# A list schedule made twice: the second pass counts due times from the first pass's tensor-engine times

## The chip, the cores and the metric

The kernel runs on one core of a Trainium2 chip. A core has a matrix engine (TensorE, "PE" in the profile; its weight loads are listed apart as "PEld"), a vector engine (DVE), a scalar engine (ACT), a general engine (POOL), and SyncE (SP), which here only issues DMA transfers. Each engine takes its own instructions in one fixed order; engines meet through semaphores. The metric is the device time in microseconds of one execution. Before the change it is 1381.08 us, the median of three runs (1380.90 to 1382.62).

## What is computed

One layer of a streaming encoder for two request groups that share weights: a prompt of 2048 rows of width 1024, and a sample batch of 8 streams with 16 new rows each, whose keys and values of 1024 past rows lie in a cache.

```
h = rms_norm(x);  z = h @ w_in                  # 1024 -> 3584 columns
u_a, v_a, g_a, q, k, v, g_b = split(z)
y_a = u_a * (tril(W_s) @ rms_norm(v_a) + b_s) * silu(g_a)     # 4 groups, chunks of 128 rows
q, k = rms_norm(q), rms_norm(k)                                # 4 heads x two halves of 64
a = softmax(q1 k1 - slope*dist) - lam * softmax(q2 k2 - slope*dist)
y_b = rms_norm(a @ v) * silu(g_b)
y = x + concat(y_a, y_b) @ w_out
```

The prompt's attention is causal in blocks of 64; the sample's sees all 1024 past rows and its own. Keys, values and the sample's v_a are outputs too.

## The kernel before, in words

All matrix products run on PE in fp32r, most of them three times: an operand is split into a rounded high part (ACT, line 481 or 648) and a low remainder (DVE, line 482 or 649), and high-high, high-low and low-high products are summed in PSUM (`mm3`, lines 491 to 494; their matmuls are recorded at line 416, transposes at line 420).

The work comes in stages, written as Python generators that are woven into one stream of instructions:

- The **main stream** (`stream`, line 771) makes the input projection: in two halves of the rows, for each of 14 blocks of weight columns, 24 matmuls of 256 columns into a tile `acc` for each 128 rows. Its rows come in through `xload` (lines 588 to 606: load, square on ACT, root on POOL, scaling on DVE at line 605) and `xpose` (transposes `x_tp`, then the split into `xT`). Its weights come in through `load_w` (lines 630 to 652): a load of 128 rows into `wraw` on SP (lines 634 to 641), a high part on ACT or POOL (line 648 or 645) and a low part on DVE (line 649). `wraw` has five buffers during the first block, `w` twelve. At the start, some forty small constants are loaded through the same SP queue: lines 463 to 468, 548 to 553 and 565 to 574.
- The **sample's attention** (`sample_attention`, line 1185) is woven into the main stream: cached keys through `skraw` (line 1103), cached values through `svraw` (line 1153), split into `sv`, which feed the products `sS` and `sO`. The loads of `svraw` have two buffers.
- **Attention A**, for the first eight row blocks of 128 (`attention`, line 990), is woven into the rest of the main stream: scores `S`, exponentials `ex` on ACT, their difference on DVE, transposes `a_tp`, a split `aT`, products `oT`.
- **Attention B**, for the other eight, is woven into the output projection `oo` (`out_stream`, line 1307), which loads `y` and `xo`. After B the last of the output projection runs alone.

The woven order in the code is not the order on the chip. At the end, `Order(tc).run()` (line 1362) takes all instructions and makes a **list schedule**. It goes through modelled time. For each engine it keeps the instructions whose inputs are ready, and takes the one with the lowest rank; `cost` (line 188) gives modelled durations, a DMA is modelled as 2.5 us plus its bytes, and buffers are taken and freed as the tiles' users finish. The order found for each engine is then fixed with dependencies (lines 394 to 397), so on the chip each engine follows it whatever happens.

The ranks come from `deadlines` (line 229). First every instruction gets a time `when`: the sum of the modelled PE durations ahead of it in the code's order, as if PE ran that order without a gap. A PE instruction's rank is that time. Any other instruction's due time starts at `when` plus 15 us (`LATE`), and then, going backwards, it is drawn to its users' due times less its own duration (3.1 us for a DMA) and a hop between engines; the reuse of a buffer counts as a user. SP's order of DMAs comes from the same ranks.

## Time and profile before

| | |
|---|---|
| median of 3 runs | 1381.08 us |
| profiled execution, its own time | 1381.83 us |
| its span, first to last instruction | 1380.1 us |
| instructions | 27913 |
| PE busy | 1347.1 us, 9892 matmuls and transposes |
| DVE, ACT, POOL busy | 925.7, 791.2, 452.1 us |
| moved by DMA | 183.05 MB, 133 GB/s in the mean |

The profiled execution lies 1.73 us above its span, and 0.75 us above the median of the runs. In the windows of time that are shown below, each engine has the time that it was busy and, in brackets, how many instructions it started; "PEclk" is the TensorE clock granted, 1.00 being full. In the list of waits, the columns are the total in us, how many, and the longest. Rows of the timeline give the start and the length of a merged group of like instructions, and in square brackets how long the engine was idle before it and what ended that.

### The profile page before, as it was taken

How to read it: one execution, taken by the hardware profiler on the slowest of the kernel's cores; microseconds unless marked ns; L12 is line 12 of the kernel's file. 1: busy time of each engine (PE TensorE's matmuls, PEld its weight loads, DVE VectorE, ACT ScalarE, POOL GpSimd, SP SyncE). 2: the span in 40 equal slices, each digit the busy share in tenths (PEclk: the TensorE clock that was granted, in tenths of full speed). 3: DMA queues.
4: the chain of work that ended last, by engine and by line, in shares of the span. 5: the costliest groups of instructions: out<-in, count | busy, mean ns of one | idle time of the engine just before them, and what ended most of it. 6: DMA issues, size and time to landing. Idle time of an engine off the chain costs nothing.

```text
span 1380.1 us, 27913 instructions
## 1 busy us (share of the span) xinstructions
PE 1347.1 (98%) x9892; PEld 1260.5 (91%) x9892; DVE 925.7 (67%) x2286; ACT 791.2 (57%) x1778; POOL 452.1 (33%) x624
## 2 busy tenths in 40 slices
PE   5999999999999999999999999999999999999998
PEld 5999999999998999899999999998788888888887
DVE  4532338878777796678889775433889897887721
ACT  4433337766565785556676654223777776776620
POOL 2151530101010121656442323021565555454400
PEclk9999999999999999999999999999999999999999
DMA  6533334554445576635453325226646543442223
GB/s 213 178 83 102 83 76 130 174 153 135 142 124 151 157 226 187 173 93 157 108 148 100 98 66 157 77 73 214 187 144 180 140 133 107 145 131 81 84 89 104
DMA packets 209244, 183.05 MB, mean 133 GB/s; under 512 B 21104, under 2 KB 167024, under 8 KB 209104
## 3 DMA queue, kind: packets, MB, share of 16 engines
q1 hardware_dynamic: 199280, 155.17, 38.1%
q0 software_dynamic: 9824, 26.09, 7.0%
q8 instruction: 78, 1.28, 0.4%
q14 instruction: 62, 0.51, 0.1%
HBM read 130.86 MB, written 42.47 MB: 126 GB/s over the span
## 4 chain that ended last, share of the span: by engine, by line
PE 89%; DMA 4%; ACT 3%; DVE 2%; issue 1%; SPq 1%; POOL 0%; ACTq 0%; DVEq 0%
PE acc L416 44%; PE oo L416 13%; PE S L416 9%; PE oT L416 7%; PE a_tp L420 4%; PE sS L416 2%; PE sk_tp L420 2%; PE sO L416 2%; PE y_tp L420 1%; DMA svraw<-in_cache_v_dram 1%; PE mix L416 1%; PE x_tp L420 1%; DMA wraw<-in_w_in_dram 1%; PE k_tp L420 1%; ACT sa L1142 1%
## 5 line engine op out<-in xcount | busy, mean ns | idle before, releaser
L416 PE MATMUL acc<-w,xT 128*128 128x256 f32 x5376 | 715.3, 283 | 3.6 <-DVE w L649 1.8
L416 PEld LDWEIGHTS acc<-w,xT 128*128 128x128 f32 x5376 | 675.6, 190 | 13.8 <-DVE w L649 2.3
L416 PE MATMUL oo<-wo,yT 128*128 128x512 f32 x816 | 231.7, 400 | 1.3 <-ACT yT L481 1.3
L416 PE MATMUL S<-kT,qT 128*128 128x512 f32 (+3 forms) x688 | 186.5, 361 | 2.2 <-DVE sst L911 2.1
L915 ACT ACTIVATE ex<-ex,sst 128x128 f32<-128x128 f32 (+15 forms) x128 | 153.9, 1203 | 41.1 <-DVE sst L911 40.2
L416 PEld LDWEIGHTS oo<-wo,yT 128*128 128x128 f32 x816 | 146.5, 188 | 26.6 <-ACT yT L481 1.8
L416 PE MATMUL oT<-aT,v 128*128 128x256 f32 x864 | 150.7, 293 | 0.2 <-ACT aT L481 0.2
L649 DVE SCALAR_TENSOR_TENSOR w<-wraw,normg,w 128x256 fp32r<-128x256 f32 x224 | 105.5, 496 | 57.9 <-ACT w L648 56.5
L911 DVE CUSTOM_DVE_ANT_0 ex<-S,dist,sst 128x512 f32<-128x512 f32 (+2 forms) x192 | 123.6, 652 | 29.0 <-PE S L416 27.8
L648 ACT ACTIVATE w<-wraw,normg 128x256 fp32r<-128x256 f32 x220 | 104.4, 505 | 57.3 <-DMA wraw<-in_w_in_dram 40.3
L416 PEld LDWEIGHTS S<-kT,qT 128*128 128x128 f32 x688 | 112.6, 189 | 18.1 <-DVE sst L911 6.1
L416 PEld LDWEIGHTS oT<-aT,v 128*128 128x128 f32 x864 | 120.8, 189 | 4.5 <-ACT aT L481 0.5
L481 ACT CAST aT<-a_tp 128x512 fp32r<-128x512 f32 (+1 forms) x144 | 79.7, 561 | 65.3 <-PE a_tp L420 63.3
L482 DVE TENSOR_TENSOR aT<-a_tp,aT 128x512 fp32r<-128x512 f32 (+1 forms) x144 | 93.6, 658 | 27.6 <-ACT aT L481 25.7
L911 DVE CUSTOM_DVE_ANT_0 ex<-S,dist 128x512 f32<-128x512 f32 (+3 forms) x128 | 79.2, 629 | 21.4 <-PE S L416 16.5
L488 POOL TENSOR_SCALAR vst<-vst 128x2 f32<-128x2 f32 (+1 forms) x36 | 9.0, 250 | 257.3 <-ACT vn L743 256.4
L420 PE MATMUL a_tp<-ident,ex 128*128 128x128 f32 x544 | 88.6, 274 | 1.3 <-DVE ex L927 0.9
L420 PEld LDWEIGHTS a_tp<-ident,ex 128*128 128x128 f32 x544 | 64.7, 140 | 13.1 <-DVE aT L482 2.5
L931 POOL TENSOR_TENSOR ex<-ex 128x1024 f32<-128x1024 f32 (+4 forms) x32 | 58.7, 1849 | 23.8 <-ACT ex L930 23.7
L482 DVE TENSOR_TENSOR sv<-svraw,sv 128x512 fp32r<-128x512 f32 (+1 forms) x72 | 50.3, 700 | 22.4 <-ACT sv L481 21.6
L481 ACT CAST sv<-svraw 128x512 fp32r<-128x512 f32 (+1 forms) x72 | 44.3, 618 | 32.6 <-DMA svraw<-in_cache_v_dram 15.0
L927 DVE SCALAR_TENSOR_TENSOR ex<-ex,sst 128x1024 f32<-128x1024 f32 (+4 forms) x64 | 62.1, 970 | 0.9
(144 smaller groups left out, 1901.1 us busy)
## 6 DMA issues: line engine op xcount, KB each, us to landing
wraw<-in_w_in_dram SPq DMA_DIRECT2D x160, 128.0 KB, 2.9
skraw<-in_cache_k_dram SPq DMA_DIRECT2D x64, 256.0 KB, 2.9
svraw<-in_cache_v_dram SPq DMA_DIRECT2D x64, 256.0 KB, 3.0
kT<-k_scr POOLq DMA_DIRECT2D x20, 512.0 KB, 5.2
vraw<-out_dram SPq DMA_DIRECT2D x36, 256.0 KB, 3.1
y<-y_scr SPq DMA_DIRECT2D x34, 256.0 KB, 2.9
out_dram<-xo SPq DMA_DIRECT2D x34, 256.0 KB, 2.2
wraw<-in_w_in_dram SPq DMA_DIRECT2D x128, 64.0 KB, 2.4
```

The source lines that it names most:

```text
L416: pe.last = nc.tensor.matmul(*a, **k).ins
L420: pe.last = nc.tensor.transpose(*a, **k).ins
L481: act.copy(hi, src)
L482: (lo_eng or dve).tensor_tensor(out=lo, in0=src, in1=f(hi), op=ALU.subtract)
L488: pool.tensor_scalar(out=ms, in0=ms, scalar1=1.0, scalar2=EPS, op0=ALU.mult, op1=ALU.add)
L648: act.activation(w[:, 0], r, AF.Copy, scale=normg[:, kc:kc + 1])
L649: dve.scalar_tensor_tensor(out=w[:, 1], in0=r, scalar=normg[:, kc:kc + 1], in1=f(w[:, 0]), op0=ALU.mult, op1=ALU.subtract)
L911: dve.tensor_tensor_reduce(out=ex[c][:, a:b], in0=s, in1=dist[:, off + a:off + b], scale=SLOPES[h], scalar=prev[c], op0=ALU.add, op1=ALU.m ...
L915: act.activation(ex[c][:, :w], ex[c][:, :w], AF.Exp, bias=prev[c], scale=-1.0, accum_out=st[:, c, 6:7])
L927: dve.scalar_tensor_tensor(out=p0, in0=p1, scalar=st[:, 1, 7:8], in1=p0, op0=ALU.mult, op1=ALU.add)
L931: pool.tensor_tensor(out=p0, in0=p1, in1=p0, op=ALU.add)
L1142: act.activation(a[r:r + 32], p[c1], AF.Copy, scale=st[c1, 6:7])
```

## The change

`Order(tc).run()` is called twice, each time on a new `Order`. The first call makes the schedule as before, keeps for every instruction the modelled time `at` at which it was taken, and returns these times instead of fixing an order. The second call gets them as `when`: a PE instruction's rank is now its modelled start in the first schedule, and every other instruction's due time starts from its own start in the first schedule plus 15 us, and is drawn back from the PE starts of the first schedule as before. Only the second schedule's order is fixed. No instruction, tile, buffer or transfer is added or removed; the costs, the slacks and the weaving are as before.

```diff
-    def deadlines(self, cost, reach):
-
-        N, t, when = self.nodes, 0.0, []
-        for n in N:
-            when.append(t)
-            if n.engine == self.PE:
-                t += cost[n.idx][1]
+    def deadlines(self, cost, reach, when):
+
+        N = self.nodes
         due = [x if n.engine == self.PE else x + self.LATE for n, x in zip(N, when)]
...
-    def run(self):
+    def run(self, when=None):
...
-        rank = self.deadlines(cost, reach)
+        first_pass = when is None
+        if first_pass:
+            t, when = 0.0, []
+            for n in N:
+                when.append(t)
+                if n.engine == self.PE:
+                    t += cost[n.idx][1]
+        rank = self.deadlines(cost, reach, when)
+        at = [0.0] * len(N)
...
-            n = N[i]
+            n, at[i] = N[i], t
...
+        if first_pass:
+            return at
...
-    Order(tc).run()
+    Order(tc).run(Order(tc).run())
```

## The prediction

> **What bounds the kernel now.** I read the page first:

> ```profile
> span 1380.1 us, 27913 instructions
> PE 1347.1 (98%) x9892; PEld 1260.5 (91%) x9892; DVE 925.7 (67%) x2286; ACT 791.2 (57%) x1778; POOL 452.1 (33%) x624
> ```

> PE sets the time. The change neither adds nor removes a PE instruction, so all it can touch is the 1380.1 - 1347.1 = 33.0 us in which PE is idle, and what short losses the busy time hides. The second view is the windows, cut by stage:

> ```profile
> 0.00:50.00 50.00, 34.70 (x242) 33.52 (x243) 23.87 (x55) 25.21 (x49) 10.83 (x29) 0.93 0.71 220
> 50.00:200.00 150.00, 150.00 (x1268) 150.00 (x1267) 57.11 (x129) 52.60 (x107) 61.69 (x64) 1.00 0.34 95
> 400.00:500.00 100.00, 97.26 (x776) 93.59 (x775) 78.90 (x194) 68.37 (x170) 13.37 (x25) 1.00 0.51 151
> 500.00:600.00 100.00, 95.44 (x749) 91.15 (x748) 66.54 (x147) 61.42 (x138) 39.95 (x52) 1.00 0.65 183
> 600.00:750.00 150.00, 150.00 (x1209) 146.52 (x1207) 128.85 (x337) 99.76 (x267) 72.60 (x118) 1.00 0.43 117
> 750.00:800.00 50.00, 48.54 (x381) 46.61 (x379) 39.61 (x110) 29.09 (x81) 14.48 (x31) 1.00 0.42 112
> 930.00:1000.00 70.00, 65.92 (x379) 54.65 (x379) 40.67 (x106) 37.29 (x67) 28.43 (x35) 1.00 0.65 202
> 1050.00:1340.00 290.00, 290.00 (x1757) 251.86 (x1757) 219.58 (x542) 190.69 (x330) 135.02 (x158) 1.00 0.42 123
> 1340.00:1380.10 40.10, 36.07 (x176) 29.18 (x174) 8.65 (x15) 4.30 (x11) 1.40 (x4) 1.00 0.28 95
> ```

> The second number is PE's busy time. Idle: 15.30 us in the first 50, 4.03 in the last 40, 2.74 and 4.56 in the sample's stage and at the start of attention A (400 to 600), 1.46 at 750 to 800, 4.08 at the turn to attention B (930 to 1000); the windows left out hold the other 0.9. Three long stretches, 590 us together, have none. The third view is what PE waited for:

> ```profile
> PE x_tp L420 <- DVE x L605: 9.3, 2, 7.2
> PE sO L416 <- ACT sv L481: 3.2, 2, 2.3
> PE x_tp L420 <- DVE neglam L474: 3.1, 1, 3.1
> PE q_tp L420 <- DMA qraw<-q_scr: 2.5, 2, 1.3
> PE S L416 <- DVE sst L911: 2.1, 4, 1.4
> PE acc L416 <- DVE w L649: 1.8, 1, 1.8
> PE acc L416 <- ACT w L648: 1.7, 1, 1.7
> ```

> They are single accidents of 1 to 3 us, each a late feed; only the first 7.2 us, until the first rows have arrived, is out of any order's reach.

> **The change, part by part.** Both passes run while the program is built, so the second costs the chip nothing, and all counts stay. What moves is the order on every engine, SP's DMA queue and POOL's included. A rank matters only against the other ranks on its engine, so the question is where the first schedule left the code's order. If it did not, the second pass repeats the first. The numbers of the instructions in the program give the code's order: 3342 of the main stream's `acc` matmuls stand ahead of the first `S` of attention A, 3381 ahead of its first `oT`. PE ran more (windows up to these two starts, `acc` alone):

> ```profile
> 0.00:566.50 566.50, 457.37 (x3437) 433.51 (x3437) 23.34 (x60) 41.01 (x98) 0.99 0.50 146
> 0.00:589.66 589.66, 475.24 (x3570) 450.16 (x3570) 23.34 (x60) 42.74 (x101) 0.99 0.50 146
> ```

> That is 95 and 189 `acc` early; at 150/1268 = 0.118 us each, 11 and 22 us. From 566 us on, everything that feeds attention A is ranked some 20 us too urgent against everything that feeds `acc`. By the same count the sample's first key transposes, at 203 us, are some 14 us behind the code. From 50 to 200, 800 to 930 and 1050 to 1340 the two orders agree within a few us. So the second pass has something to correct at three places.

> **(a) The head.** The code puts the transposes of row tiles 0 to 3 ahead of the first `acc`. The chip did otherwise:

> ```profile
> 9.31 0.47 SPq L548 DMA_DIRECT2D qkg<-in_q_norm_g_dram  x1
> 9.39 1.13 POOL L645 TENSOR_SCALAR w<-wraw,normg 128x256 fp32r<-128x256 f32 x2 [0.57 <-DMA wraw<-in_w_in_dram]
> 12.10 0.69 DVE L482 TENSOR_TENSOR xT<-x_tp,xT 128x512 fp32r<-128x512 f32 x1 [1.30 <-ACT xT L481]
> 13.22 0.35 SPq L593 DMA_DIRECT2D x<-in_x_prompt_dram  x1
> 14.37 2.06 DVE L649 SCALAR_TENSOR_TENSOR w<-wraw,normg,w 128x256 fp32r<-128x256 f32 x5
> 14.95 3.51 SPq L553 DMA_DIRECT2D bias_s<-in_sgu_b_dram  x4
> 16.19 4.43 PE L416 MATMUL acc<-w,xT 128*128 128x256 f32 x29
> 22.60 0.43 SPq L574 DMA_DIRECT2D ws<-in_sgu_w_dram  x1
> 23.14 1.40 SPq L634 DMA_DIRECT2D wraw<-in_w_in_dram  x3
> 23.73 1.06 PE L420 MATMUL x_tp<-ident,x 128*128 128x128 f32 x8 [3.10 <-DVE neglam L474]
> 26.54 0.79 PE L416 MATMUL acc<-w,xT 128*128 128x256 f32 x2 [1.75 <-ACT w L648]
> ```

> The first five weight tiles carry 29 `acc` at 16.19; then PE starves, first for row tile 3 (3.10 us), then for weight tiles 5 to 7 (1.75 us). Those are issued only at 23.14: their buffers come free when line 649 has read the first five (14.37 to 16.43), and eleven constants stand in front. From 9.31 to 23.03 SP issued 19 constants and two row tiles, 0.65 us each on the chip against the schedule's 0.40. In the first pass tiles 0 to 3 outrank these weights throughout; in the second the weights are due by the first pass's `acc`, which runs before tile 3. Line 649 can then go ahead of the row tiles' work on DVE, from 10.52 (the end of the POOL row) at the earliest, up to 3.85 us sooner. I take half of that, 1.9 us, which is 4 or 5 places in the schedule's SP queue, some 3 us on the chip: the 1.75 us vanish. After this gap PE also ran slow:

> ```profile
> 26.00:28.00 2.00, 1.46 (x7) 1.47 (x8) 1.75 (x4) 0.48 (x1) 0.47 (x1) 0.50 0.81 232
> 28.00:30.00 2.00, 2.00 (x11) 2.00 (x10) 1.46 (x3) 1.47 (x3) 0.10 (x1) 0.50 0.90 268
> 30.00:32.00 2.00, 2.00 (x13) 2.00 (x13) 1.18 (x3) 1.95 (x4) 0.67 (x2) 0.61 0.80 287
> 32.00:34.00 2.00, 2.00 (x19) 2.00 (x19) 1.15 (x3) 0.00 (x0) 0.08 (x1) 1.00 0.88 328
> ```

> 24 matmuls between 28 and 32 instead of 38: 14 x 0.105 = 1.5 us, and about 0.5 more before 28; 2.0 us hang on the gap, of which I take half. [...] Head: -1.75 - 1.0 = **-2.8 us**. Bounds: -6.9 if both waits and the slow clock go (3.10 + 1.75 + 2.0); +3.5 if four more constants like the `bias_s` row get ahead of a load that PE needs, which the changed due time of constants (their own early start plus 15 us, instead of the place in the code plus 15 us) could do.

> **(b) Attention A, 560 to 800.** PE's 1.8 us wait for a weight tile falls there, beside waits of attention itself (`S`, `q_tp`). The re-ranking should remove most of the first and may lengthen the others: **-1.6**, bounds -6.0 (all of the 4.56 and 1.46) and +2.3 (one new wait as long as the longest for `sv`). Attention, now less urgent, may fall further behind, but its scores end well before the main stream; first row `S`, second `acc`:

> ```profile
> 850.00:900.00 50.00, 0.00 (x0) 0.00 (x0) 0.00 (x0) 1.00 0.31 89
> 900.00:950.00 50.00, 36.74 (x307) 36.49 (x305) 1.25 (x3) 4.32 (x10) 1.00 0.49 158
> ```

> Some 50 us and more of `acc` hide a later end; without them each us of lag would cost up to one.

> **(c) The turn to attention B.** 4.08 us idle, from four kinds of wait; by the count, the output stream runs ahead of the code there by up to 20 us. I take a quarter, **-1.0**, bounds -4.1 and +2.3.

> **(d) New accidents in the sample's stage.** Here SP's order decides:

> ```profile
> 423.35 1.37 SPq L762 DMA_DIRECT2D y_scr<-ya  x3
> 424.82 0.85 SPq L1153 DMA_DIRECT2D svraw<-in_cache_v_dram  x2
> 428.59 0.50 PE L416 MATMUL sO<-sv,saT 128*128 128x512 f32 x1 [2.32 <-ACT sv L481]
> ```

> One value load issued behind stores costs PE 2.32 us. Ranks between weights, stores and sample loads shift by up to the 14 us above at the stage's start and by little later. A third of the 9.2 us of four such accidents, less the 1.6 that may as well go: **+1.4**, bounds -3.2 and +9.2.

> Sum: -2.8 - 1.6 - 1.0 + 1.4 = -4.0 us. Against the profiled execution, 1381.83 - 4.0 = 1377.8; it lay 0.75 above the median, so 1377.1 us in the terms of the runs: **1377**.

> **The rivals.** *No change* (1381, within 2.8 us, which is 0.2% and about what this kernel's runs can tell): the re-ranking stays inside slack. For it: 590 us without idle, ACT 57% and DVE 67% busy, twelve `w` buffers. Its extreme is that the second schedule repeats the first in all but the three places and the accidents there merely change names. *More than forecast* (about 1369): the head's whole 6.9 and half of the idle in (b) and (c), 5.1, go; against it, PE waited for tile 3 until 23.73 though its load had gone out at 13.22, as soon as a buffer was free, and an order can hardly issue it sooner. *Slower, by the sample's loads* (1387): where the sample is behind the code, its loads lose rank to weights and stores; SP's queue is strict, `svraw` has two buffers, and each load issued 4 us late costs 2.3 us. Four such make +9.2, less 3 of the gains: +6. It decides from three new waits on; one in the trace shows that the stage is open to it, and that only few of the 64 cache loads hit PE speaks against. [...] *Slower, by the head's constants* (1385): the +3.5 above decides if it also meets the slow clock.

> **How the numbers follow.** Forecast, 1371 to 1378: 0.40. More than forecast: 0.08. No change: 0.24. Slower by the sample's loads: 0.18; by the head: 0.10. So faster 0.48, same 0.24, slower 0.28. The range runs from the middle of the larger gain, with all of (a) and most of (b) and (c), 1367, to the slower rival with one more wait, 1388; the likeliest case's own is 1371 to 1378.

> **What would show it.** (a): weight tiles 5 to 7 issued before 21 us, PE's idle in the first 50 us at 12 to 13.5 instead of 15.3, fewer rows at 0.50. (b): no wait for `w` after 50 us; `acc` counts ahead of the first `S` as before or higher. (c): idle at 930 to 1000 of 3 us or less. (d): `sO` waits in all at most 5 us. The forecast is wrong if the head's idle doesn't shrink, or if the waits for `sv`, `skraw` and `qraw` together exceed 10 us.

## The result, and the profile after

The changed kernel is slower. Six runs of it have a median of 1386.15 us (1384.58 to 1388.45), six of the kernel before beside them 1381.85 us (1377.54 to 1386.02): a ratio of 1.0037, with a 95% interval of 1.0023 to 1.0051. A second set of twelve runs gave 1384.35 us and 1.0028 (1.0017 to 1.0040). The profiled execution took 1386.94 us, 5.1 more than that of before. The time lies inside the predicted range, but the direction is wrong: 1377 was forecast, with a chance of 0.28 for slower.

The head of the page comes first, then the windows of the changed kernel by the stages of the prediction (span of the window, busy time and count of PE, PEld, DVE, ACT, POOL, granted clock, DMA share, GB/s):

```profile
span 1385.1 us, 27894 instructions
PE 1351.8 (98%) x9892; PEld 1264.1 (91%) x9892; DVE 929.2 (67%) x2286; ACT 790.0 (57%) x1778; POOL 448.2 (32%) x624
```

```profile
0.00:50.00 50.00, 35.33 (x249) 34.00 (x250) 24.55 (x63) 25.49 (x49) 10.66 (x29) 0.97 0.72 220
200.00:300.00 100.00, 98.88 (x781) 94.00 (x780) 80.00 (x217) 68.59 (x172) 6.52 (x12) 1.00 0.47 136
400.00:500.00 100.00, 98.04 (x780) 93.92 (x779) 78.88 (x195) 69.09 (x172) 13.82 (x25) 1.00 0.51 152
500.00:600.00 100.00, 99.00 (x782) 94.79 (x782) 66.86 (x143) 60.38 (x135) 37.84 (x48) 1.00 0.64 185
600.00:750.00 150.00, 147.02 (x1173) 142.59 (x1172) 124.76 (x324) 93.63 (x255) 69.34 (x117) 1.00 0.45 118
750.00:800.00 50.00, 49.98 (x405) 48.78 (x404) 40.43 (x111) 30.27 (x87) 15.71 (x33) 1.00 0.39 103
930.00:1000.00 70.00, 63.37 (x334) 52.89 (x333) 37.62 (x95) 34.38 (x62) 25.13 (x30) 0.94 0.60 192
```

PE's idle time is 1385.1 - 1351.8 = 33.3 us, as good as unchanged (33.0). What grew is the "busy" time, by 4.7 us for the same 9892 instructions: PE was slower while busy. Between these two profiles the idle time has also moved. From 500 to 600 it fell from 4.56 to 1.00 us (782 instructions in the window where there were 749), from 750 to 800 from 1.46 to 0.02; but 600 to 750, which had none, now has 2.98 (1173 instead of 1209), and the turn at 930 to 1000 went from 4.08 to 6.63, with a granted clock of 0.94 in place of 1.00.

From the list of what PE waited for, changed kernel (total, times, longest):

```profile
PE x_tp L426 <- DVE x L611: 9.4, 2, 7.2
PE a_tp L426 <- DVE ex L933: 4.3, 2, 3.0
PE x_tp L426 <- DVE neglam L480: 2.6, 1, 2.6
PE acc L422 <- ACT w L654: 2.0, 2, 1.7
PE sO L422 <- ACT sv L487: 2.0, 3, 1.5
PE a_tp L426 <- DVE gbt L990: 1.4, 1, 1.4
PE oT L422 <- ACT aT L487: 1.2, 2, 1.0
```

The waits for `qraw` and for `w` from DVE are gone from the list; behind the wait for the first rows a new one leads, `a_tp` for `ex`, 4.3 us in two. (Line numbers behind the diff are six higher than before.)

**The turn.** The timeline of PE there, first of the kernel before, then of the changed one:

```profile
966.39 2.34 PE L416 MATMUL oo<-wo,yT 128*128 128x512 f32 x9
970.03 0.41 PE L420 MATMUL q_tp<-ident,qraw 128*128 128x128 f32 x2 [1.30 <-DMA qraw<-q_scr]
971.04 1.06 PE L420 MATMUL a_tp<-ident,ex 128*128 128x128 f32 x8 [0.60 <-DVE ex L927]
976.79 1.07 PE L416 MATMUL S<-kT,qT 128*128 128x512 f32 x4
```

```profile
964.79 2.30 PE L422 MATMUL oo<-wo,yT 128*128 128x512 f32 x9
970.08 0.41 PE L426 MATMUL a_tp<-ident,ex 128*128 128x128 f32 x2 [3.00 <-DVE ex L933]
970.50 0.41 PE L426 MATMUL q_tp<-ident,qraw 128*128 128x128 f32 x2
978.23 2.86 PE L422 MATMUL oT<-aT,v 128*128 128x256 f32 x17
981.41 1.18 PE L422 MATMUL S<-kT,qT 128*128 128x512 f32 x4
995.19 0.66 PE L422 MATMUL S<-kT,qT 128*128 128x128 f32 x4 [0.72 <-DVE sst L917]
998.68 1.93 PE L426 MATMUL a_tp<-ident,ex 128*128 128x128 f32 x8 [1.31 <-DVE ex L933]
```

The nine `oo` start 1.60 us **ahead** of before (964.79 against 966.39): up to here the change has gained. The next unit's scores `S` start 4.62 us **behind** (981.41 against 976.79). Between these two points the changed kernel has fallen back by 6.2 us; its span ended 5.0 later. The two orders differ: before, the query transposes `q_tp` ran first and the `a_tp` behind them; now the first `a_tp` run ahead of them, and the `S` that the queries feed stand behind seventeen `oT`. PE found nothing to do for 3.00 us in one piece, where it had waited 1.30 and 0.60. Narrow windows of the changed kernel show what followed:

```profile
970.00:972.00 2.00, 1.67 (x11) 1.21 (x11) 1.47 (x4) 1.05 (x3) 1.29 (x2) 0.85 0.07 17
972.00:974.00 2.00, 1.85 (x8) 1.56 (x9) 1.54 (x3) 1.24 (x3) 0.59 (x1) 0.50 1.00 276
974.00:976.00 2.00, 2.00 (x11) 2.00 (x11) 0.59 (x1) 0.59 (x1) 1.88 (x3) 0.50 0.62 170
976.00:978.00 2.00, 2.00 (x12) 2.00 (x11) 0.56 (x2) 0.80 (x2) 0.43 (x1) 0.50 0.35 68
1000.00:1002.00 2.00, 2.00 (x11) 2.00 (x10) 2.00 (x5) 0.96 (x2) 1.12 (x2) 0.50 0.42 88
```

From 971.4 to 978.2 the tensor clock is half: 6.83 us, which cost half of that, 3.4 us, as PE was busy nearly throughout. A second spell, 3.41 us, follows the 1.31 us wait at 998. In the profile of before no row of the turn is below 1.00. So of the 6.2 us: 3.24 - 2.48 = 0.8 is idle time (3.00 and 0.24, against 1.30, 0.60, 0.34 and 0.24), 3.4 is half clock, and the remaining 2.0 is, by this subtraction, `S` standing further back in the order, which is a shift and no loss by itself. Idle time and half clock together are the loss: 4.2 us up to `S`, and 1.7 more in the second spell.

**The head** is where the prediction saw its largest gain. Timeline of the changed kernel, SP and PE:

```profile
23.10 1.39 SPq L640 DMA_DIRECT2D wraw<-in_w_in_dram  x3
23.71 1.07 PE L426 MATMUL x_tp<-ident,x 128*128 128x128 f32 x8 [2.61 <-DVE neglam L480]
26.46 0.79 PE L422 MATMUL acc<-w,xT 128*128 128x256 f32 x2 [1.69 <-ACT w L654]
```

The same three rows, at the same times to 0.1 us, as before. The second plan has the same order in the head as the first: on every engine the two plans are identical up to 216 us of modelled time. The better clock of the window, 0.97 where before had 0.93, is not the change's doing either: a second profile of the changed kernel has 0.93 there.

### The profile page after: what moved, and what is told of

Read it like the earlier page. It is cut to its first block, busy times and chain, and to the rows that moved or that the text cites. A ratio compares the mean times of both kernels' runs of the same rounds, so it can differ in the third digit from the quotient of the medians.

```text
span 1385.1 us, 27894 instructions
## 1 busy us (share of the span) xinstructions
PE 1351.8 (98%) x9892; PEld 1264.1 (91%) x9892; DVE 929.2 (67%) x2286; ACT 790.0 (57%) x1778; POOL 448.2 (32%) x624
## 3 DMA queue, kind: packets, MB, share of 16 engines
q8 instruction: 78, 1.28, 0.4%
## 5 line engine op out<-in xcount | busy, mean ns | idle before, releaser
L422 PE MATMUL oT<-aT,v 128*128 128x256 f32 x864 | 154.3, 297 | 1.7 <-ACT aT L487 1.2
L655 DVE SCALAR_TENSOR_TENSOR w<-wraw,normg,w 128x256 fp32r<-128x256 f32 x224 | 110.2, 519 | 53.9 <-ACT w L654 51.8
L426 PE MATMUL a_tp<-ident,ex 128*128 128x128 f32 x544 | 91.8, 278 | 6.2 <-DVE ex L933 4.3
```

What stands on the lines that cost most here:

```text
L422: pe.last = nc.tensor.matmul(*a, **k).ins
L426: pe.last = nc.tensor.transpose(*a, **k).ins
L655: dve.scalar_tensor_tensor(out=w[:, 1], in0=r, scalar=normg[:, kc:kc + 1], in1=f(w[:, 0]), op0=ALU.mult, op1=ALU.subtract)
```

## The experiments

Theory at the outset: the turn's new order makes a gap, and the gap costs clock. The rivals: the loss comes from some other part of the new order, or from half-clock spells that come and go whatever the order. All times below are medians, all ratios are to runs of the kernel before beside them, with 95% intervals.

### The changed kernel once more

No edit.

> The changed kernel once more, beside the others of this call. Clock theory: the loss comes from spells of half TensorE clock that follow idle stretches of PE at the turn to attention B (two spells, 6.8 and 3.4 us long, in the first profile: 3.4 + 1.7 us lost), while the idle sums of both kernels are equal (33.0 and 33.3 us); so 3 to 6 us over the kernel before, with half-clock spells between 960 and 1010 us in every profile. Idle theory: the loss is the idle time itself, at the turn (4.1 to 6.6 us) and within attention A (0 to 3.0 us); the same time, 3 to 6 us over.

Measured: 1384.35 us (1382.86 to 1389.24 in twelve runs), 1.0028 (1.0017 to 1.0040). The loss is real. The spread of 6.4 us goes mostly with the clock: the run at 1389.24 had a mean granted clock of 0.991, the one at 1382.86 had 0.998. Over the 18 runs of the changed kernel, time rises by 0.6 us for each us that the clock withholds (mean clock off 1.00, times the run's length; correlation 0.79). But the mean clocks of the two kernels hardly differ: 0.9951 here and 0.9957 over 96 runs of before, 0.8 us withheld. At 0.6 that makes 0.5 us of the mean difference of 3.8. Of runs with the same mean clock, 0.996, seven of the changed kernel average 1384.1 us and 31 of before 1380.5. The pair of first profiles overstates the clock's share: that of before has no spell at the turn, which need not hold for its other executions (a run below bears on that).

### Work in the gap

Sixteen matmuls that nothing reads are put on PE ahead of the first `a_tp` of the two units at the turn, eleven and five; PE is then busy where it waited. They add some 3.6 us of PE work (the row of the eleven is 2.65 us long, that of the five 1.31).

```diff
...
             tp = bank("tr", "a_tp")
+            if kk == 0 and FILLS.get("n"):
+                for _ in range(FILLS["n"].pop(0)):
+                    pe.matmul(tp, lhsT=wo[0][0][:, 0, 0:P], rhs=wo[0][0][:, 0], start=True, stop=True)
...
```

> The changed kernel's order, and 11 and 5 useless matmuls of 512 columns (about 2.5 and 1.1 us of PE work) put in front of the first a_tp of attention B's first and second unit, where PE stands idle for 3.0 and 1.3 us; their results are overwritten. All other engines' orders are the same, instruction by instruction. Clock theory: with the gaps filled PE's clock stays up, and 3.4 to 5.1 us come back although PE does 3.6 us more work: 1380 to 1383, no half-clock spell between 960 and 1010. Idle theory: the fill lies in time that is lost anyway: 1385 to 1388, no gain.

Measured: 1383.00 us, 1.0016 (1.0007 to 1.0026). PE has more to do, and the kernel is 1.35 us shorter than without it. Its windows:

```profile
930.00:1000.00 70.00, 65.74 (x368) 54.62 (x367) 41.52 (x105) 36.53 (x66) 26.29 (x32) 1.00 0.61 192
1000.00:1050.00 50.00, 49.98 (x313) 43.64 (x312) 43.04 (x114) 37.32 (x74) 27.52 (x36) 1.00 0.45 132
```

The clock stays at 1.00 through the turn, and the mean clock of the runs rises from 0.9951 to 0.9977. So the gap does cost clock; yet less came back than the 3.4 to 5.1 us expected, and the kernel remains 0.16% slower than before.

The same edit was made in the kernel before, with its one pass:

> The kernel before with the 11 and 5 useless matmuls of the filled kernel in front of the same a_tp. If its turn, too, loses clock in part of the runs: mean granted clock up from 0.9956 to 0.997 or more, and the time grows by 2 us or less though PE does 3.6 us more. If the kernel before loses no clock there: clock unchanged, 1383 to 1385.

Measured: 1381.74 us, 1.0010 (0.9998 to 1.0021), with the clock at 1.00 at the turn in its profile. There the same 3.6 us of extra work cost next to nothing: it fills waits that are there anyway, and the mean clock of the runs rises from 0.9957 to 0.9970, as was expected if before, too, loses clock at its turn in part of its runs. Its one profile shows no such spell, but those of two kernels below whose turn has short waits like its own (the main stream's times alone, and the first pass's idle alone) have lost clock there: 0.98 at 930 to 1000 in both, about what one spell of 3.41 us at half clock makes of 70 us (1.7 us withheld). The four means side by side: before 1381.4, before filled 1382.0; changed 1385.2, changed filled 1383.1. With both turns filled, 1.1 us of the 3.8 us are left. About 2.7 us of the loss hang on the gaps at the turn, and about 1.1 are elsewhere (the new idle time at 600 to 750 among it, less the gain at 500 to 600); the standard error of each is 0.6 to 0.8 us.

### One half of the feedback

The last `acc` divides the program: the main stream, and all behind it (attention B and the output). First, only the main stream's instructions take their times from the first pass; the others keep the code's time, moved by one constant, `shift`. It is 18.12 us: so much later than in the code's sum stands the last `acc` in the first plan (14.93 us of modelled idle time in the head, 3.19 near 550 us).

```diff
...
+            cut = 1 + max(n.idx for n in N if n.engine == self.PE and n.writes[0].bass_ap.tensor.name.startswith("acc"))
+            shift = max(w for n, w in zip(N[:cut], when) if n.engine == self.PE) - code[cut - 1]
+            when = [w if (i < cut) == True else c + (0.0 if i < cut else shift) for i, (w, c) in enumerate(zip(when, code))]
```

> The second pass takes the first pass's times only for instructions up to the main stream's last acc, and from there the code order's times, moved by one constant. Clock theory: the turn is as in the kernel before, without half-clock spells there; of the second pass stay the shorter idle at 500 to 600 and 750 to 800 (-4.9 us) and the longer one at 600 to 750 (+3.0): 1378 to 1382. If the loss sat in attention A: 1384 to 1387, as long as the changed kernel.

Measured: 1379.01 us, 0.9988 (0.9978 to 0.9998). The turn has the old order again (`q_tp` waits 1.17 us for its load, then `a_tp` 0.78 for `ex`). The gain at 500 to 600 is there (98.98 busy), and half of the loss at 600 to 750:

```profile
600.00:750.00 150.00, 148.53 (x1189) 144.47 (x1188) 124.20 (x331) 96.04 (x256) 68.83 (x112) 1.00 0.44 119
930.00:1000.00 70.00, 66.17 (x364) 54.60 (x363) 43.48 (x113) 39.16 (x70) 28.14 (x33) 0.98 0.60 188
```

Then only the part behind the main stream:

```diff
...
+            when = [w if (i < cut) == False else c + (0.0 if i < cut else shift) for i, (w, c) in enumerate(zip(when, code))]
```

> The reverse: the code order's times up to the main stream's last acc, the first pass's times from there. Clock theory: the turn has the changed kernel's gaps and its half-clock spells: 1384 to 1388. If the loss sat in attention A: 1380 to 1382, as the kernel before.

Measured: 1381.06 us, 0.9997 (0.9986 to 1.0008); expected was a loss, so this missed. Its waits and windows:

```profile
PE a_tp L435 <- DVE ex L942: 4.3, 2, 3.0
```

```profile
500.00:600.00 100.00, 98.76 (x782) 94.88 (x781) 69.15 (x157) 63.49 (x146) 41.02 (x54) 1.00 0.65 189
600.00:750.00 150.00, 150.00 (x1208) 146.66 (x1207) 127.52 (x335) 99.95 (x267) 71.09 (x118) 1.00 0.45 123
930.00:1000.00 70.00, 62.99 (x339) 52.73 (x338) 41.08 (x104) 36.22 (x64) 26.23 (x32) 0.95 0.61 188
```

The turn's waits are there in full, to the tenth: 4.3 us in two, 3.0 the longest, clock 0.95. So they come from the times fed back to attention B. But this kernel has the gain at 500 to 600 as well (98.76 busy against 95.44), and not the loss at 600 to 750, although every instruction of the main stream has the code's time. In both kernels the second part is due later, against the first, than in the kernel before (in the last one by 18.1 us, where the main stream's own PE ranks move by 14.9 in the median). The due times that the kernel's own planner works out show how that reaches the main stream here: through chains of buffers, 573 of the 3624 instructions off PE that stand ahead of the last `acc` move 4.57 us later, while 3019 of them and all PE ranks there stay as they were.

### The 4.56 us alone

One pass, the code's times, and 4.56 us added to everything behind the last `acc`, in the kernel before. In the planner's due times this does to the main stream what the last experiment did: 575 instructions move by 4.56 us, and 3019 stay.

```diff
+        cut = 1 + max(n.idx for n in N if n.engine == self.PE and n.writes[0].bass_ap.tensor.name.startswith("acc"))
+        when = [w if i < cut else w + 4560.0 for i, w in enumerate(when)]
```

> One pass, code order's times, but everything behind the main stream's last acc is moved 4.56 us later, the gap that the first pass leaves there. It makes the main stream's supporting work, whose due times hang on that through chains of buffers, less urgent against the attention's, and leaves the turn as in the kernel before. If the changed kernel's loss is made by second-pass times at the turn, and its gain at 500 to 600 and 750 to 800 by the shift that these times contain: -3 to -6 us, 1376 to 1379, idle at 500 to 800 under 3 us, the turn as before. If that gain needs the second pass: as the kernel before, 1380 to 1383.

Measured: 1376.86 us, 0.9974 (0.9964 to 0.9984), as expected. (4.56 us is, to 0.01, the move that the fed-back times gave these due times. The expectation calls it a gap that the first pass leaves behind the last `acc`; the first plan has none of that length there.) Its windows:

```profile
500.00:600.00 100.00, 99.11 (x785) 95.26 (x784) 68.82 (x155) 62.57 (x142) 40.91 (x53) 1.00 0.67 191
600.00:750.00 150.00, 149.51 (x1203) 145.76 (x1201) 127.72 (x335) 99.54 (x265) 70.48 (x117) 1.00 0.45 122
930.00:1000.00 70.00, 66.63 (x365) 54.75 (x365) 45.74 (x120) 41.79 (x75) 31.02 (x36) 0.98 0.56 174
```

The gain at 500 to 600 is whole, without the losses at 600 to 750 and at the turn. No second pass is needed for it. How 4.56 us behind the main stream can move work at 560 us: due times are drawn back through the reuse of buffers, and such chains lead from attention B's and the output's tiles back to the gates, evictions and weights of the main stream.

### A longer lead ahead of the turn

The output stream gets a longer lead before attention B is woven in (`OB` 12 for 9), so that more `oo` are at hand at the turn. With two passes:

```diff
-OB, OT = 9, 6
+OB, OT = 12, 6
```

> The changed kernel with the output projection led by 12 instead of 9 us of PE work before attention B goes on. If the turn's idle comes from PE running out of output work ahead of attention B's first a_tp: the 3.0 us gap shrinks below 1.5, fewer half-clock spells at 960 to 1010 (mean clock 0.996 or more), 1379 to 1382. If only B's own chain counts, the time stays at 1384 to 1386.

Measured: 1378.86 us, 0.9987 (0.9976 to 0.9997), 5.5 us below the twelve runs of the changed kernel; the longest wait for `ex` fell from 3.0 to 2.3 us and became the only one. The wait is longer than the 1.5 us expected, and the time at the good end: the lead gains twice the 2.7 us of the turn's gaps, and why it gains the rest stays open. And the same lead with one pass (the kernel before with `OB` 12):

> The kernel before, one pass, with the same lead of 12 us. A control for the lead alone: 1380 to 1383, within 1.5 us of the kernel before, since its turn loses less there. If the lead helps one pass as much as two, it is 1377 or less, and the lead has nothing to do with the second pass.

Measured: 1381.68 us, 1.0008 (0.9996 to 1.0020): nothing. The lead helps the second pass and gives nothing without it.

### What in the fed-back times does it

Three kernels with two passes, in which `code` is the code's time stretched by the idle time of the first pass, so that the first pass's idle is kept and its reordering is left out. First, every instruction gets that time:

```diff
...
+            for n in sorted((n for n in N if n.engine == self.PE), key=lambda n: when[n.idx]):
+                xs.append(done)
+                ys.append(when[n.idx])
+                done += cost[n.idx][1]
+            code = [float(c) for c in np.interp(code, xs, ys)]
+            when = [c for w, c in zip(when, code)]
```

> Two passes; the second gets the code order's times, only stretched by the idle time that the first schedule gave PE (an instruction's time is the first schedule's time at which PE had done as much work as stands ahead of it in the code). No instruction's own displacement enters. If the changed kernel's gain is in the idle, and its two losses (within attention A at 600 to 750, and at the turn) come from the displacements: -2 to -6 us, 1376 to 1380, idle at 600 to 750 under 1 us, the turn as in the kernel before. If the losses come with any second pass: 1384 or more.

Measured: 1381.41 us, 0.9996 (0.9985 to 1.0006). A miss: the turn's waits are near those of before (`q_tp` 1.0 us, `a_tp` 0.9), and 500 to 600 has its gain (98.75 busy), but 1.45 us came back as idle at 600 to 750, and the gain expected over the whole is not there.

Then the earlier of the two times, so that nothing is forgiven for having been late:

```diff
+            when = [min(w, c) for w, c in zip(when, code)]
```

> Two passes; each instruction's time is the earlier of its own start in the first schedule and its stretched place in the code: what ran ahead of the code keeps that as its new time, what ran late is not allowed its lateness. Lateness theory (an instruction that was late in the first pass gets the late time as its due time, so the chain behind it loses urgency just where it was late): no loss at 600 to 750 and at the turn, 1377 to 1382. Earliness theory (the main stream's early matmuls become too urgent): the 4 us of loss at 600 to 750 stay, 1383 to 1387.

Measured: 1381.87 us, 1.0005 (0.9996 to 1.0015). And the later of the two, so that lateness is forgiven and an early start is not pressed:

```diff
+            when = [max(w, c) for w, c in zip(when, code)]
```

> The reverse: the later of the two. Lateness theory: both losses are there, 3 us and more of idle at 600 to 750 and a turn of 12 us or more of lost time, 1384 to 1389. Earliness theory: no loss at 600 to 750, the time within 2 us of the kernel before.

Measured: 1386.37 us, 1.0034 (1.0023 to 1.0045). Windows, "earlier" first, then "later":

```profile
500.00:600.00 100.00, 97.25 (x754) 93.37 (x753) 68.43 (x157) 62.87 (x144) 36.24 (x48) 0.98 0.64 184
600.00:750.00 150.00, 149.65 (x1206) 146.57 (x1205) 126.20 (x330) 96.54 (x258) 75.56 (x119) 1.00 0.47 124
930.00:1000.00 70.00, 66.15 (x371) 55.26 (x371) 38.32 (x99) 34.89 (x63) 27.83 (x35) 0.98 0.64 200
```

```profile
500.00:600.00 100.00, 95.45 (x742) 90.27 (x741) 67.77 (x149) 61.64 (x141) 37.66 (x46) 1.00 0.63 185
600.00:750.00 150.00, 150.00 (x1211) 146.96 (x1210) 120.87 (x320) 94.11 (x255) 72.12 (x117) 1.00 0.46 124
930.00:1000.00 70.00, 63.88 (x354) 53.91 (x353) 37.82 (x97) 34.13 (x62) 26.73 (x34) 0.96 0.64 197
```

At the turn the two go opposite ways: 3.85 us idle where late instructions keep their old due time, 6.12 where their lateness becomes their due time, with the loss of the whole kernel back. In "later" the waits aren't the same as in the changed kernel, though (`q_tp` 2.1 us for DVE's `qT`, then `a_tp` 1.2), so it shows the direction, not the same accident. Nor is its whole loss at the turn: it lacks the gain at 500 to 600 (95.45 busy, as before). At 600 to 750 neither kernel has the loss; it needs both the lateness and the early starts, or another thing. Its cause stays open.

### The best of them

Attention B's times from the second pass, the code's times for the main stream, and the longer lead:

```diff
-OB, OT = 9, 6
+OB, OT = 12, 6
...
+            when = [w if (i < cut) == False else c + (0.0 if i < cut else shift) for i, (w, c) in enumerate(zip(when, code))]
```

> The code order's times up to the main stream's last acc, the first pass's from there (as in the run that did this alone), with the lead of 12 us. If the two findings add (attention A without the second pass's loss, the turn covered by the longer lead): 1375 to 1378, as fast as the shift alone or faster. If the lead only trades one stall for another at the end of attention B: 1378 to 1381.

Measured: 1374.42 us (1374.01 to 1376.03 in five runs), 0.9952 (0.9937 to 0.9967). It beats both kernels, by 6.8 us the one before, and is a little better than the 1375 to 1378 expected. Windows:

```profile
500.00:600.00 100.00, 99.47 (x791) 95.95 (x790) 69.34 (x157) 62.69 (x143) 40.72 (x53) 1.00 0.68 192
600.00:750.00 150.00, 149.47 (x1201) 145.75 (x1200) 127.61 (x335) 99.51 (x265) 70.56 (x117) 1.00 0.45 122
930.00:1000.00 70.00, 65.98 (x358) 56.20 (x357) 42.85 (x111) 38.80 (x70) 28.97 (x33) 0.95 0.59 182
```

It takes the gain at 500 to 600, not the loss at 600 to 750, and its turn has 4.02 us of idle, at a granted clock of 0.95.

## Why the prediction was wrong, point by point

**(a) The head, -2.8 us: wrong, nothing moved.** The step that failed is "in the second the weights are due by the first pass's `acc`, which runs before tile 3". They are not: due times in the head are drawn back through chains of buffers from far behind it. In the planner's ranks the load of weight tile 5 goes from -57.2 us in the first pass to -39.0 in the second, that of row tile 3 from -65.4 to -47.3. Both move by the 18.1 us by which the last `acc` is late in the first plan, so their order stays. The three weight loads were issued at 23.10 us where 21 was the bound, and the two waits (2.61 and 1.69) stand where they stood. The 0.6 us by which the window's idle fell (15.30 to 14.67) can't be put down to the change: it comes with an order that is the same in this stage. That 1.0 us of slow clock would go with the gap was an estimate that no run shows: the waits stayed, and the window's clock was 0.93 before, 0.97 and 0.93 in two profiles of the changed kernel. The planner is not blind to such waits, either: it has 14.9 us of idle time in the head in both passes, near the chip's. Counting due times anew does not remove a wait if everything around it moves by the same amount.

**(b) Attention A, -1.6 us: the size is near by luck, the cause is not the one given.** Idle over 500 to 800 fell by 6.02 - 4.00 = 2.0 us, and the wait of `acc` for `w` from DVE is gone, as it was to show (one of 0.3 us for `w` from ACT is left). But this is a gain of 5.0 less a new loss of 2.98 at 600 to 750, in waits of attention itself (`a_tp` for `gbt` 1.4, `oT` for `aT` 1.0 and 0.4). The prediction had allowed for such waits, up to 2.3 us: attention did become less urgent (its ranks at 600 to 800 move by some 40 us, those of the weights beside it by 18.1) and fell behind (3677 `acc` ahead of its first `oT` instead of 3570). The kernel with the main stream's times alone has half of this loss, the one without them none. The gain does not need the 11 to 22 us by which PE runs ahead of the code: the one-pass kernel with 4.56 us has it without any time of the first pass. And single profiles overstate it: the kernel before with its turn filled, whose PE order is that of before up to the turn, had 2.11 and 0.28 us of idle at 500 to 600 and 750 to 800, where before had 4.56 and 1.46.

**(c) The turn, -1.0 us: this step failed, and it decided.** The mark was 3 us of idle or less at 930 to 1000; it is 6.63. The bound of +2.3 held one new wait as long as the longest for `sv`; the idle grew by 2.55, a little past it, and the clock, priced in the head alone, was not priced here at all. The pair of profiles puts `S` 6.2 us further back; over many runs, where before pays some clock at its turn as well, the filled kernels put 2.7 on the gaps. The mechanism in the plan: in the first pass the second unit's query load arrives late, so its `q_tp` waits, and the query's copies on POOL run behind. With the code's times that chain is overdue, and it goes ahead of everything. The planner's own ranks (no times of the chip) have the query's splits on DVE at 905 to 906 us in the first pass, against 914 for the step that combines `ex`; in the second at 943 to 944, against 941. What was 8 us more urgent is 2 us less urgent: the delay of the first pass has become the due time of the second. So `ex` and the first `a_tp` overtake the queries, PE meets them before they are ready, and the next `S` comes late. By the same reckoning the second plan ends 0.8 us later than the first, with 10.0 us of idle at the turn instead of 7.4. That attention B's fed-back times bring this about is shown (with these times alone the wait is the same to the tenth, without them the old order is back); that it is the lateness in them is supported by the "earlier" and "later" kernels, which differ elsewhere too, and not proved.

**(d) The sample's stage, +1.4 us: about nothing.** The waits of `sO` came to 2.0 us (3.2 before), idle at 400 to 500 fell by 0.78, and at 200 to 300 it rose by 0.92 (99.80 busy before). The rival that has this stage as its place did not come about.

**The rivals.** Slower by the sample's loads (1387) came near the time, by another road: no new wait there. Slower by the head's constants: no; their due times did come forward, but stayed behind those of the loads that PE needs. That the second schedule repeats the first was true of the plan's first 216 us. The remark that the time ends within 0.2% of before if re-ranking stays inside slack failed at the one place where there is no slack, the turn, of which the prediction only said "I take a quarter", without asking which chain was overdue.

**The marks.** That the head's idle doesn't shrink was named as what would make the forecast wrong; it shrank by 0.6 us where 1.8 to 3.3 were forecast. Of the marks of the parts, the turn's missed (6.63 us of idle for at most 3), that of attention A came but for a wait of 0.3 us for `w`, and that of the sample's stage came.

## What to carry to other kernels

Feeding a schedule its own start times can forgive what was late in it: an overdue chain loses the urgency by which it recovered. Feed back only what is a property of a stage (an offset of 4.56 us at its border was worth 0.26% here by itself), and look first at the turns between stages, where no other work covers a new wait. And compare the plans themselves before running anything. Against the plan of before, by the planner's own modelled times, that of the changed kernel ends 0.8 us later, that with 4.56 us alone 3.2 earlier, "later" 4.6 later, the best of them 4.2 earlier; the measured means lie 3.8 above, 4.3 below, 5.0 above and 6.5 below. Over the kernel before and the ten changed ones without filling, the two agree with a correlation of 0.92. The plan does not have the clock, and misses by up to 3 us, but it had the sign of this change.

## What was not expected of the hardware

**A vector operation slowed beside POOL.** The step that the 3.00 us wait was for, changed kernel, DVE and POOL, and the same step before:

```profile
967.60 1.26 POOL L488 TENSOR_TENSOR v<-vraw,v 128x512 fp32r<-128x512 f32 x1 [0.56 <-ACT v L487]
967.73 2.21 DVE L933 SCALAR_TENSOR_TENSOR ex<-ex,sst 128x1024 f32<-128x1024 f32 x1
```

```profile
969.61 1.28 DVE L927 SCALAR_TENSOR_TENSOR ex<-ex,sst 128x1024 f32<-128x1024 f32 x1
970.49 1.54 POOL L482 TENSOR_TENSOR v<-vraw,v 128x512 fp32r<-128x512 f32 x1
```

The same operation took 2.21 us where POOL had started a subtraction 0.13 us earlier, and 1.28 where POOL began later; there it was POOL's that took longer, 1.54 for 1.26. So 0.93 us of the gap come with what the new order put side by side. The ranks don't hold this; the planner's modelled time does keep two such operations apart (`port`), but only each engine's own order is fixed on the chip, not how the two engines meet. The operation took 2.21 to 2.23 us in all four profiles with the changed turn, and 1.28 or 1.29 in those of before, of the 4.56 us alone and of the main stream's times alone. With one pass and the longer lead it took 2.14. That POOL's operation is what delays DVE's is a reading of these rows; the pairing itself was not tried by a run of its own.
